# A two-layer diffusion trunk: token statistics of keys and queries apart, the scan's gate in its own pool, the attention's pools moved

## The chip, the cores and the metric

The kernel runs on one core of a Trainium2 chip. The metric is the device time of one execution in microseconds, as the median of the runs. A core has five engines that work through a queue of instructions each, in order: TensorE (PE: matmuls), VectorE (DVE), ScalarE (ACT), GpSimd (POOL) and SyncE (SP), which here only issues DMAs. They wait for one another by semaphores. GpSimd and ScalarE issue DMAs too.

## What is computed

Two layers of a trunk over 640 tokens: 512 latent tokens and 128 context tokens. Cut to the parts that the change touches:

```python
def trunk_layer(x, mod, p, ctx):
    h = modulate(x, shift1, scale1)            # RMS norm, scale, shift
    z = h @ p['w_in']                          # one projection, split by columns
    y_a = mixer_ssm(z[ssm])                    # A: state-space scan, both ways
    q = rmsnorm(rmsnorm(c_q) @ w_uq)           # B: low-rank queries, per-head norm, rotary
    k, v = rmsnorm([rmsnorm(ckv) @ w_uk, k_rope]), rmsnorm(ckv) @ w_uv
    y_b = softmax(q k^T) v
    y_c = mixer_gmlp(z[gmlp])                  # C: mixing within chunks of 128
    x = x + gate1 * (norm([y_a, y_b, y_c]) @ w_out)
    x = x + gate2 * conv_ffn(modulate(x, shift2, scale2))

def mixer_ssm(u):                              # ... scan -> y
    y = gelu(y + d * u)
    return y * sigmoid(y @ ssm_w_glu)
```

The two rmsnorms of `c_q` (256 wide) and `ckv` (128 wide) give one scale for each token. These are the "token statistics": a sum of squares over the width, and its inverse square root.

## The kernel before

The whole trunk is one program on one core. An activation is kept transposed, channels on the partitions and the 640 tokens (642 columns with two of padding) along the free dimension, and cut in two halves of 322 and 320 columns. Matmuls are made of three passes (`whi*hh`, `whi*hl`, `wlo*hh`): ScalarE casts a weight tile to its high part `whi` (L117), VectorE subtracts for the low part `wlo` (L118). Each layer has two stretches: the mixers (0 to 464 us and 1010 to 1340) and the FFN (464 to 1010 and 1340 to 1800).

No order is written out by hand. A scheduler of the framework takes the program, simulates it, and lays down one fixed instruction order for each engine. Tiles live in pools; a pool opened where another was closed reuses its memory, and its first writes wait until the last readers and writers of what lay there are done. Each layer has two sides of the memory, `sa` and `sb`, on which pools are stacked.

The end of the mixer stretch, in the order of the code:

- The scan, in four quarters (`ssm_quarter`, once for each quarter of the channel groups). For each, GpSimd's queue loads its tables (`T` L692, `we` L690, `tp` L696, `qt` L694), GpSimd copies the state into `E` (L724, L727), VectorE scans (`m`, `H`, `hq`, L744 to L763), TensorE forms `y` (L775 to L777), ScalarE copies it to `ys` (L779), and SP stores it with two DMAs to `Yd` in memory (L781).
- The gate (`ssm_output`), in the scan's pool: it loads `yT`, transposed, back from `Yd` with 16 DMAs, 8 on SP and 8 on GpSimd in turn (L800), and for both halves `t` of its 256 channels takes a square on ScalarE (`ga`, L811), two operations on VectorE (L812, L813), a tanh (L814), one more on VectorE (L815) and two copies to `gl` (L819). Then TensorE multiplies by `wg` (`glu`, L824), ScalarE takes a tanh (`th`, L828), and VectorE writes `yA` (L829, L830).
- The projection for the attention, in the pool `prj` on side `sa`: `put_c` evicts three blocks of the input projection (`win`): for the keys' block (m = 4) `ckh`, `ckl`, `sqk`, for the queries' two (m = 2, 3) `cqh` (L977), `cql` (L978), `sqq` and `sq` (L980). Ten one-column matmuls `tst` (L1008) give the token sums; VectorE makes `v` (L1011, L1012), one inverse square root of 10 columns (`rsqrt`, L102 to L111), and two copies into `sc` (L1014, L1016).
- Six key/value tiles: TensorE `kv` (L1036 to L1038), ScalarE copies `ks` (L1040), squares `hsq` (L1042) and writes `Vt` scaled by `sc` (L1044); VectorE reduces `ms` (L1043). Then the key norms (L1151 to L1166), five query tiles `q` (L1055 to L1062) and the query norms, whose last product is L1189.
- The attention, in pools `att` and `actx` on side `sb`: transposes `kt`, `qt`, the casts `kh` (L1236) and `kl` (L1237), maxima `mx`, scores and values. In between TensorE works off the matmuls of the modulation (`mod`, L261), whose weights SP loads (`raw<-w_mod`, L258).

## Time and profile before

| what | us |
|---|---|
| median of 3 runs (1825.23 to 1832.4) | 1825.25 |
| the profiled execution | 1826.58 |
| its span | 1824.8 |
| TensorE busy | 1694.3 (93%) |
| VectorE busy | 1156.8 (63%) |
| ScalarE busy | 679.8 (37%) |
| GpSimd busy | 312.8 (17%) |
| TensorE busy in 0 to 464 (mixers, layer 0) | 387.85 of 464 |
| in 464 to 1010 (FFN, layer 0) | 535.58 of 546 |
| in 1010 to 1340 (mixers, layer 1) | 293.93 of 330 |
| in 1340 to 1800 (FFN, layer 1) | 457.48 of 460 |

A busy share is an average over stages: in the FFNs TensorE is nearly never idle, in the mixers it is at times. A row of a timeline gives start, duration, and in brackets the idle time before it and what ended it. The span is what the profiler sees of one execution, and the execution's own time is 1.78 us longer.

### The profile page before, as it was taken

The numbers are of one execution on the slowest core, as the hardware profiler recorded it, in microseconds if no ns is written. First come the engines' busy times: TensorE is split into PE (matmuls) and PEld (weight loads), VectorE is DVE, ScalarE is ACT, GpSimd is POOL, SyncE is SP. The second block draws the span as 40 slices with busy tenths as digits, with TensorE's granted clock in tenths as the row PEclk, the third lists the DMA queues.
The fourth block names the chain that finished last, engine by engine and source line by source line (L and its number), as shares of the span: only waits on it lengthen the run. The fifth ranks groups of instructions, "written<-read, shape, count | busy, mean of one in ns | idle before, by whom it ended". The sixth has DMA issues, their size and how long they took to land.

```text
span 1824.8 us, 28970 instructions
## 1 busy us (share of the span) xinstructions
PE 1694.3 (93%) x11248; PEld 1512.6 (83%) x11248; DVE 1156.8 (63%) x2421; ACT 679.8 (37%) x1210; POOL 312.8 (17%) x738
## 2 busy tenths in 40 slices
PE   5878889999989999999999888999989999999998
PEld 3767755468889999999999876455989999999998
DVE  6887875667674646556477568566786464555564
ACT  4334454433452414224244346343344232332241
POOL 2886200000086060540000120000000000000000
PEclk7889789899899999999999978999989999999999
DMA  9265453301443523234132633540223131331221
GB/s 281 84 174 148 124 162 123 110 15 56 129 137 118 170 56 116 59 94 116 35 90 67 164 105 107 167 133 1 70 70 93 36 104 47 93 92 36 82 82 58
DMA packets 217577, 182.48 MB, mean 100 GB/s; under 512 B 33438, under 2 KB 202204, under 8 KB 217440
## 3 DMA queue, kind: packets, MB, share of 16 engines
q1 hardware_dynamic: 194736, 154.33, 28.2%
q0 software_dynamic: 8272, 23.87, 4.4%
q10 hardware_dynamic: 14432, 2.44, 0.7%
q8 instruction: 89, 1.46, 0.3%
q14 instruction: 48, 0.39, 0.1%
HBM read 161.94 MB, written 18.64 MB: 99 GB/s over the span
## 4 chain that ended last, share of the span: by engine, by line
PE 75%; DVE 10%; DMA 7%; ACT 4%; POOL 2%; issue 2%; ACTq 1%; SPq 0%; DVEq 0%; POOLq 0%
PE up L141 11%; PE up L143 11%; PE up L142 11%; PE dn L142 6%; PE dn L141 6%; PE dn L143 6%; PE o L1287 3%; PE mod L261 2%; DMA raw<-w_mod 2%; PE wo L141 1%; PE wo L143 1%; PE wo L142 1%; DMA raw<-ffn_w_up 1%; PE s L1267 1%; PE win L141 1%
## 5 line engine op out<-in xcount | busy, mean ns | idle before, releaser
L141 PE MATMUL up<-hh,whi 128*128 128x322 f32 x1408 | 435.6, 315 | 8.8 <-ACT hh L357 7.9
L143 PE MATMUL up<-hh,wlo 128*128 128x322 f32 x1408 | 440.9, 314 | 1.1 <-DVE wlo L118 1.0
L142 PE MATMUL up<-hl,whi 128*128 128x322 f32 x1408 | 439.7, 313 | 1.6 <-DVE hl L358 1.5
L141 PEld LDWEIGHTS up<-hh,whi 128*128 128x128 f32 x1408 | 266.1, 191 | 14.3 <-ACT hh L357 7.2
L142 PEld LDWEIGHTS up<-hl,whi 128*128 128x128 f32 x1408 | 268.8, 191 | 2.6 <-DVE hl L358 2.6
L143 PEld LDWEIGHTS up<-hh,wlo 128*128 128x128 f32 x1408 | 267.9, 190 | 2.9 <-DVE wlo L118 1.9
L118 DVE TENSOR_TENSOR wlo<-raw,whi 128x1024 fp32r<-128x1024 f32 (+1 forms) x116 | 146.7, 1266 | 142.2 <-ACT whi L117 141.0
L142 PE MATMUL dn<-glo,dh 128*128 128x322 f32 (+1 forms) x704 | 218.5, 312 | 0.2 <-DVE glo L118 0.2
L143 PE MATMUL dn<-gh,dl 128*128 128x322 f32 (+1 forms) x704 | 217.9, 311 | 0.0
L141 PE MATMUL dn<-gh,dh 128*128 128x322 f32 (+1 forms) x704 | 209.4, 312 | 4.5 <-DVE xT L1501 2.9
L1501 DVE SCALAR_TENSOR_TENSOR xT<-dn,mod,xT 128x320 f32<-128x320 f32 (+2 forms) x288 | 112.2, 435 | 129.5 <-PE dn L143 129.3
L117 ACT CAST whi<-raw 128x1024 fp32r<-128x1024 f32 (+1 forms) x116 | 120.5, 1040 | 151.1 <-PE up L142 56.8
L1532 ACT ACTIVATE cv<-up,prm,cw 128x321 f32<-128x321 f32 x88 | 54.3, 619 | 252.5 <-PE up L143 252.3
L141 PEld LDWEIGHTS dn<-gh,dh 128*128 128x128 f32 x704 | 131.0, 190 | 5.3 <-DVE xT L1501 3.1
L142 PEld LDWEIGHTS dn<-glo,dh 128*128 128x128 f32 x704 | 133.2, 189 | 0.5 <-DVE glo L118 0.5
L143 PEld LDWEIGHTS dn<-gh,dl 128*128 128x128 f32 x704 | 133.5, 190 | 0.0
L1533 DVE SCALAR_TENSOR_TENSOR cv<-up,cw,cv 128x320 f32<-128x320 f32 x88 | 48.3, 549 | 67.5 <-ACT cv L1532 67.5
L261 PE MATMUL mod<-raw,sT 128*32 128x256 f32 x768 | 64.5, 431 | 27.1 <-DMA raw<-w_mod 24.8
L118 DVE TENSOR_TENSOR dl<-raw,dh 128x1024 fp32r<-128x1024 f32 x44 | 54.0, 1227 | 45.8 <-ACT dh L117 45.6
L117 ACT CAST dh<-raw 128x1024 fp32r<-128x1024 f32 x44 | 46.1, 1047 | 56.8 <-DMA raw<-ffn_w_down 50.1
L261 PEld LDWEIGHTS mod<-raw,sT 128*32 128x32 f32 x768 | 19.5, 114 | 57.5 <-DMA raw<-w_mod 29.2
L1250 DVE TENSOR_REDUCE nml<-mx 128x1 f32<-128x640 f32 x64 | 50.9, 820 | 24.0 <-PE mx L1248 23.7
(472 smaller groups left out, 3422.5 us busy)
## 6 DMA issues: line engine op xcount, KB each, us to landing
raw<-w_mod SPq DMA_DIRECT2D x96, 512.0 KB, 4.6
raw<-ffn_w_up SPq DMA_DIRECT2D x88, 512.0 KB, 4.1
raw<-ffn_w_down SPq DMA_DIRECT2D x44, 512.0 KB, 3.5
raw<-w_in SPq DMA_DIRECT2D x10, 512.0 KB, 5.7
we<-WEd POOLq DMA_DIRECT2D x8, 512.0 KB, 4.1
qt<-Qd POOLq DMA_DIRECT2D x8, 512.0 KB, 5.1
raw<-w_out SPq DMA_DIRECT2D x16, 256.0 KB, 5.1
raw<-w_out SPq DMA_DIRECT2D x8, 512.0 KB, 3.4
```

What stands on the lines that cost most here:

```text
L117: self.nc.scalar.copy(hi, raw)
L118: self.nc.vector.tensor_tensor(lo, raw, hi.bitcast(F32), op=OP.subtract)
L141: mm(ps, wh, xh, start=start, stop=False)
L142: mm(ps, wh, xl, start=False, stop=False)
L143: mm(ps, wl, xh, start=False, stop=stop)
L261: nc.tensor.matmul(ps[j * 32:j * 32 + 32, c0:c0 + 256], self.sT[:, k0 + j, :], rv[:, j, :], start=k0 == 0, stop=k0 == 4)
L1250: V.tensor_reduce(nm[:, tt:tt + 1], pb[:, :, :320], axis=AX.XY, op=OP.max, negate=True)
L1267: mm(ps, kh[i][:, kc_], qh[i], start=True, stop=False)
L1287: mm(pb[i * 64:(i + 1) * 64, 0], Vt[:, kt, 2 * p + i], Ps[i][kt], start=kt == 0, stop=kt == 4)
L1501: self.nc.vector.scalar_tensor_tensor(self.xT[:, m, a:b], po[:, a - lo:b - lo], self.modcol(l, gi, m, c), self.xT[:, m, a:b], op0=OP.mult, ...
L1532: A.activation(z[:, 0:321], po[:, 0:321], AF.Identity, bias=b, scale=c1)
L1533: V.scalar_tensor_tensor(z[:, 1:321], po[:, 0:320], c0, z[:, 1:321], op0=OP.mult, op1=OP.add)
```

## The change

1. `rsqrt` makes its first guess with one operation, a multiplication of the bits by -0.5, in place of a shift and a multiplication. It takes an engine for its three Newton steps; GpSimd needs four operations for a step where VectorE needs three.
2. `token_scales` takes the place of the ten matmuls and the one call: keys and queries have five matmuls, a `v` and a first guess on VectorE each, and 12 Newton operations and one copy into `sc` on GpSimd each, right behind their blocks of the projection.
3. The gate gets a pool of its own, `so`, opened after the scan's pool is closed. Its code is called right after the scan in both layers; the tanh is written in place.
4. `att` and `actx` lie on the other side of the memory, `sa`, over `prj`.

```diff
@@ -95,20 +95,25 @@
         eng.tensor_tensor(o_re, o_re, t[0], op=OP.subtract)
         eng.tensor_tensor(o_im, o_im, t[1], op=OP.add)
 
-    def rsqrt(self, v, n):
-        nc = self.nc
-        sh = self.smt([128, n], f"rs_sh{n}", I32)
-        nc.vector.tensor_scalar(sh, v.bitcast(I32), 1, None, op0=OP.logical_shift_right)
-        y0 = self.smt([128, n], f"rs_y0{n}", I32)
-        nc.vector.tensor_scalar(y0, sh, -1.0, float(0x5F3759DF), op0=OP.mult, op1=OP.add)
+    def rsqrt(self, v, n, E=None):
+        E = E or self.nc.vector
+        n_ = f"{n}" if E is self.nc.vector else f"{n}p"
+        y0 = self.smt([128, n], f"rs_y0{n_}", I32)
+        self.nc.vector.tensor_scalar(y0, v.bitcast(I32), -0.5, float(0x5F3759DF), op0=OP.mult, op1=OP.add)
         cur = y0.bitcast(F32)
-        t = self.smt([128, n], f"rs_t{n}")
-        y = self.smt([128, n], f"rs_y{n}", bufs=3)
+        t = self.smt([128, n], f"rs_t{n_}")
+        y = self.smt([128, n], f"rs_y{n_}", bufs=3)
         for _ in range(3):
-            nc.vector.tensor_tensor(t, cur, cur, op=OP.mult)
-            nc.vector.scalar_tensor_tensor(t, t, -0.5, v, op0=OP.mult, op1=OP.mult)
-            nc.vector.scalar_tensor_tensor(y, t, 1.5, cur, op0=OP.add, op1=OP.mult)
+            E.tensor_tensor(t, cur, cur, op=OP.mult)
+            if E is self.nc.vector:
+                E.scalar_tensor_tensor(t, t, -0.5, v, op0=OP.mult, op1=OP.mult)
+                E.scalar_tensor_tensor(y, t, 1.5, cur, op0=OP.add, op1=OP.mult)
+            else:
+                E.tensor_tensor(t, t, v, op=OP.mult)
+                E.tensor_scalar(t, t, -0.5, 1.5, op0=OP.mult, op1=OP.add)
+                E.tensor_tensor(y, t, cur, op=OP.mult)
             cur = y
         return y
 
@@ -795,24 +800,23 @@
 
         nc, V, I = self.nc, self.nc.vector, self.I
         n = 8 * NC
-        y = pool.tile([128, 2, 8, NC], F32, name=self.uid("yT"), tag="uT", bufs=1)
+        y = pool.tile([128, 2, 8, NC], F32, name=self.uid("yT"), tag="yT", bufs=1)
         for g in range(16):
             (nc.gpsimd if g % 2 else nc.sync).dma_start(
                 out=y[(g % 8) * 16:(g % 8) * 16 + 16, g // 8],
                 in_=self.Yd[l][g].rearrange("(i c) k -> c i k", c=16))
-        wg = pool.tile([128, 2, 256], F32, name=self.uid("wg"), tag="tp", bufs=1)
+        wg = pool.tile([128, 2, 256], F32, name=self.uid("wg"), tag="wg", bufs=1)
         nc.sync.dma_start(out=wg, in_=I["ssm_w_glu"][l].rearrange("(t p) n -> p t n", t=2))
-        g = [pool.tile([128, NT], F32, name=self.uid("gl"), tag=tg, bufs=1) for tg in ("E", "R")]
+        g = [pool.tile([128, NT], F32, name=self.uid("gl"), tag=tg, bufs=1) for tg in ("g0", "g1")]
         for t in range(2):
             yv = y[:, t].rearrange("p i k -> p (i k)")
             nc.gpsimd.memset(g[t][:, 512:CX], 0.0)
-            a = pool.tile([128, n], F32, name=self.uid("ga"), tag="m1", bufs=1)
-            b = pool.tile([128, n], F32, name=self.uid("gb"), tag="m2", bufs=1)
+            a = pool.tile([128, n], F32, name=self.uid("ga"), tag="ga", bufs=1)
             nc.scalar.activation(a, yv, AF.Square)
             V.tensor_scalar(a, a, 0.044715, 1.0, op0=OP.mult, op1=OP.add)
             V.tensor_tensor(a, a, yv, op=OP.mult)
-            nc.scalar.activation(b, a, AF.Tanh, scale=math.sqrt(2.0 / math.pi))
-            V.scalar_tensor_tensor(a, b, 1.0, yv, op0=OP.add, op1=OP.mult)
+            nc.scalar.activation(a, a, AF.Tanh, scale=math.sqrt(2.0 / math.pi))
+            V.scalar_tensor_tensor(a, a, 1.0, yv, op0=OP.add, op1=OP.mult)
             av = a.rearrange("p (i k) -> p k i", i=8)
             for k0, k1, c in ((0, 64, 0), (65, 81, CX)):
                 o = g[t][:, c:c + 8 * (k1 - k0)].rearrange("p (k i) -> p k i", i=8)
@@ -824,7 +828,7 @@
                     nc.tensor.matmul(ps[s][:, :hi - lo], wg[:, t, m * 128:(m + 1) * 128],
                                      g[t][:, lo:hi], start=t == 0, stop=t == 1)
             for s, (lo, hi) in enumerate(((0, 320), (320, NT))):
-                th = pool.tile([128, 322], F32, name=self.uid("th"), tag="H", bufs=1)
+                th = pool.tile([128, 322], F32, name=self.uid("th"), tag="th", bufs=1)
                 nc.scalar.activation(th[:, :hi - lo], ps[s][:, :hi - lo], AF.Tanh, scale=0.5)
                 V.tensor_scalar(th[:, :hi - lo], th[:, :hi - lo], 1.0, 0.5, op0=OP.add, op1=OP.mult)
                 V.tensor_tensor(yA[:, m, lo:hi], th[:, :hi - lo], g[m][:, lo:hi], op=OP.mult)
@@ -931,7 +935,6 @@
                 self.ssm_quarter(l, q, ssm, tables or self.ssm_load(l, q, ssm), U, st, hq)
                 tables = None
             self.ssm_states(l, st)
-            self.ssm_output(l, ssm, yA)
 
         if l > 0:
             scans(tables)
@@ -954,6 +957,9 @@
             tb_ctx.close()
             self.params(1)
             scans(None)
+        ssm_ctx.close()
+        with tc.tile_pool(name=f"so{l}", bufs=1, side=sb) as so:
+            self.ssm_output(l, so, yA)
 
 
         vt = late.enter_context(tc.tile_pool(name=f"vt{l}", bufs=1, side=sa))
@@ -988,11 +994,26 @@
                 if s == 1:
                     A.activation(ckx, po[:, CX - lo:NT - lo], AF.Copy, scale=g)
 
+        def token_scales(sq, width, o, nm):
+            ps = self.pa("tst")
+            for i in range(5):
+                nc.tensor.matmul(ps[:, i:i + 1], sq[:, TOK[i]:TOK[i] + 128], self.ones[:, 0:1],
+                                 start=True, stop=True)
+            v = self.smt([128, 5], nm)
+            V.tensor_scalar(v, ps[:, 0:5], 1.0 / width, EPS, op0=OP.mult, op1=OP.add)
+            CH.tensor_copy(sc[:, o:o + 5], self.rsqrt(v, 5, CH))
+        CH = nc.gpsimd
+        CH.memset(sc[:, 5:6], 1.0)
         for m in (4, 2, 3):
             w = in_load(m)
             for s in range(2):
                 in_half(m, w, s, put_c)
+            if m == 4:
+                token_scales(sqk, 128, 6, "vk")
         V.tensor_tensor(sqq, sqq, sq2, op=OP.add)
+        token_scales(sqq, 256, 0, "vq")
 
         cc = pt("cc", [128, 128])
         nc.sync.dma_start(out=cc, in_=I["cache_ckv"][0, l])
@@ -1001,19 +1022,6 @@
         self.tr(ps[:, :128], cc)
         A.copy(ckh[:, :128], ps[:, :128])
         V.tensor_tensor(ckl[:, :128], ps[:, :128], ckh[:, :128].bitcast(F32), op=OP.subtract)
-        ps = self.pa("tst")
-        for i in range(5):
-            for j, s in enumerate((sqq, sqk)):
-                nc.tensor.matmul(ps[:, j * 5 + i:j * 5 + i + 1], s[:, TOK[i]:TOK[i] + 128],
-                                 self.ones[:, 0:1], start=True, stop=True)
-        v = self.smt([128, 10], "v10")
-        V.tensor_scalar(v[:, 0:5], ps[:, 0:5], 1.0 / 256, EPS, op0=OP.mult, op1=OP.add)
-        V.tensor_scalar(v[:, 5:10], ps[:, 5:10], 1.0 / 128, EPS, op0=OP.mult, op1=OP.add)
-        r10 = self.rsqrt(v, 10)
-        V.tensor_copy(sc[:, 0:5], r10[:, 0:5])
-        V.memset(sc[:, 5:6], 1.0)
-        V.tensor_copy(sc[:, 6:11], r10[:, 5:10])
 
         ps = self.pa("ckvo")
         self.tr(ps[:, :128], ckx)
@@ -1066,13 +1074,12 @@
         for _ in range(5):
             next(fill, None)
         prj.close()
-        ssm_ctx.close()
 
 
         yb = late.enter_context(tc.tile_pool(name=f"yb{l}", bufs=1, side=sa))
         yB = yb.tile([128, 4, NT], F32, name=self.uid("yB"), tag="yB")
         with ExitStack() as es:
-            at = es.enter_context(tc.tile_pool(name=f"att{l}", bufs=1, side=sb))
+            at = es.enter_context(tc.tile_pool(name=f"att{l}", bufs=1, side=sa))
             yh, yl = self.attention(l, M, yb, at, es, qs, ks, Vt, yB, yA, yc, ssc, fill)
         FH = self.later.enter_context(tc.tile_pool(name=f"fh{l}", bufs=1, side=sb))
         n2 = ExitStack()
@@ -1294,7 +1301,7 @@
             yield
 
 
-        with self.tc.tile_pool(name=f"actx{l}", bufs=1, side=self.sides[1]) as cx:
+        with self.tc.tile_pool(name=f"actx{l}", bufs=1, side=self.sides[0]) as cx:
             qc, kc = t("qc", [104, 8, 128], pool=cx), t("kc", [104, 8, 128], pool=cx)
             nc.sync.dma_start(out=kc[96:104].rearrange("p h c -> p (h c)"), in_=self.I["k_onehot"])
             for src, dst, g in ((qs[:, 4], qc, qg), (ks[:, 5], kc, kg)):
```

ScalarE in layer 1, where the third block's first half (320 columns) has been evicted; `cqh` and `sq` belong to the projection, `ga`, `gb` and `gl` to the gate, `ks` to the key/value tiles. Before:

```order
L977 ACTIVATE cqh_11114<-win_11251,prm_2004 128x320
L980 ACTIVATE sq_1657_11121<-win_11251 128x320
L811 ACTIVATE ga_10759<-yT_10737 128x648
L1040 COPY ks_11352<-kv_11382 128x8x64
L117 CAST whi_11484<-raw_11483 128x768
L977 ACTIVATE cqh_11114<-win_11251,prm_2004 128x322
```

and now:

```order
L983 ACTIVATE cqh_11112<-win_11275,prm_1998 128x320
L815 ACTIVATE ga_11059<-yT_11037 128x648
L986 ACTIVATE sq_1644_11119<-win_11275 128x320
L818 ACTIVATE ga_11059<-ga_11059 128x648
L823 ACTIVATE gl_11056<-ga_11059 128x512
L823 ACTIVATE gl_11056<-ga_11059 128x128
L122 CAST whi_11499<-raw_11498 128x768
L983 ACTIVATE cqh_11112<-win_11275,prm_1998 128x322
L815 ACTIVATE ga_11068<-yT_11037 128x648
```

The gate's square now stands ahead of `sq`, and the first key/value eviction has moved behind the whole gate.

SP in layer 1, around the last `Yd` stores (`x2`: two in a row). Before:

```order
L781 DMA Yd_306<-ys_10651 128x2x81 x2
L134 DMA raw_11489<-w_uq 128x768
L800 DMA yT_10737<-Yd_306 16x8x81 x2
L781 DMA Yd_306<-ys_10727 128x2x81 x2
L791 DMA out_new_ssm_re<-sto_10733 32x64
L791 DMA out_new_ssm_im<-sto_10733 32x64
L800 DMA yT_10737<-Yd_306 16x8x81 x6
```

and now:

```order
L786 DMA Yd_306<-ys_10648 128x2x81 x2
L139 DMA raw_11504<-w_uq 128x768
L786 DMA Yd_306<-ys_10724 128x2x81 x2
L796 DMA out_new_ssm_re<-sto_10730 32x64
L796 DMA out_new_ssm_im<-sto_10730 32x64
L805 DMA yT_11037<-Yd_306 16x8x81 x8
```

Two loads that stood ahead of the last stores stand behind them.

GpSimd in layer 0, between quarters 2 and 3 of the scan (`rs_t5p`, `rs_y5p`, `vq`: the queries' Newton steps). Before:

```order
L692 DMA T_2259<-Td_290 128x656
L767 COPY st_706<-hq_2028 128x2x2
L727 COPY E_2265<-h_117 128x4
L767 COPY st_706<-hq_2028 128x2x2
L696 DMA tp_2263<-Wd_298 128x512
L694 DMA qt_2261<-Qd_282 128x1024
```

and now, the last Newton step and what follows:

```order
L109 TENSOR_TENSOR rs_t5p_2641<-rs_y5p_2642 128x5
L114 TENSOR_TENSOR rs_t5p_2641<-rs_t5p_2641,vq_2637 128x5
L115 TENSOR_SCALAR rs_t5p_2641<-rs_t5p_2641 128x5
L116 TENSOR_TENSOR rs_y5p_2642<-rs_t5p_2641,rs_y5p_2642 128x5
L1005 COPY sc_703<-rs_y5p_2642 128x5
L701 DMA tp_2257<-Wd_298 128x512
L699 DMA qt_2255<-Qd_282 128x1024
L732 COPY E_2259<-h_117 128x4
```

The Newton chain has come ahead of the `tp` and `qt` loads of quarter 3, and the copy into `E` has moved behind them.

## Rows read from the trace of the kernel before

**Rows 1.** Windows: length, busy us of each engine, clock, DMA share, GB/s.
```profile
560.00:970.00 410.00, 409.20 (x2879) 403.23 (x2877) 232.37 (x403) 138.74 (x208) 100.70 (x180) 1.00 0.31 91
1080.00:1100.00 20.00, 16.55 (x54) 13.18 (x55) 11.42 (x35) 12.83 (x24) 0.00 (x0) 0.66 0.12 40
```

**Rows 2.** SP's timeline in layer 1: start, us, instruction, [idle before <-releaser].
```profile
1069.56 0.89 SPq L781 DMA_DIRECT2D Yd<-ys  x2
1071.50 5.34 SPq L800 DMA_DIRECT2D yT<-Yd  x6
```

**Rows 3.** GpSimd's timeline in layer 1.
```profile
1075.15 1.05 POOL L800 DMA_DIRECT2D yT<-Yd  x2 [3.11 <-DMA Yd<-ys]
1106.53 0.52 POOL L1214 MEMSET ql<- 1x512 f32 x1 [30.33 <-DVE ms L1153]
```

**Rows 4.** DMA issues, 1060 to 1080: count, KB each, median us to landing.
```profile
yT<-Yd POOLq DMA_DIRECT2D x8, 40.5 KB, 4.8
```

**Rows 5.** The tile yT in layer 1, its 16 loads.
```profile
DMA to landing us min/median/max: 1.9/4.5/5.5
```

**Rows 6.** ScalarE's timeline in layer 1.
```profile
1077.95 0.75 ACT L811 ACTIVATE ga<-yT 128x648 f32<-128x648 f32 x1 [2.02 <-DMA yT<-Yd]
...
1083.29 1.43 ACT L819 ACTIVATE gl<-ga 128x512 f32<-128x512 f32 x2 [0.36 <-DVE ga L815]
...
1095.02 0.58 ACT L1040 COPY ks<-kv 128x512 f32<-128x512 f32 x1 [5.08 <-PE kv L1038]
...
1103.80 0.60 ACT L1042 ACTIVATE hsq<-kv 128x512 f32<-128x512 f32 x1
1104.29 0.69 ACT L1044 ACTIVATE Vt<-kv,sc 128x512 f32<-128x512 f32 x1
```

**Rows 7.** TensorE's timeline in layer 1.
```profile
1075.97 0.41 PE L141 MATMUL win<-hh,whi 128*128 128x322 f32 x1 [0.27 <-ACT sq L980]
...
1082.98 0.80 PE L1036 MATMUL kv<-whi,ckh 128*128 128x512 f32 x1 [3.19 <-ACT sq L980]
```

**Rows 8.** VectorE's timeline in layer 1.
```profile
1107.12 0.58 DVE L102 TENSOR_SCALAR rs_sh<-ms 128x48 int32<-128x48 int32 x1
...
1121.25 0.75 DVE L1237 SCALAR_TENSOR_TENSOR kl<-kt,kg,kh 96x512 fp32r<-96x512 f32 x1
...
1135.96 0.68 DVE L1189 TENSOR_TENSOR qs<-qx,qx 128x512 f32<-128x512 f32 x1
1138.11 0.69 DVE L1358 TENSOR_TENSOR ac<-ac,msq 128x512 f32<-128x512 f32 x1 [1.46 <-ACT msq L1357]
```

**Rows 9.** GpSimd's timeline in layer 0.
```profile
200.31 0.19 POOL L727 COPY E<-h 128x4 f32<-128x4 f32 x1 [0.42 <-ACT E L720]
...
204.14 0.54 POOL L696 DMA_DIRECT2D tp<-Wd  x1 [3.52 <-PE y L775]
...
218.31 0.53 POOL L800 DMA_DIRECT2D yT<-Yd  x1 [1.21 <-DMA Yd<-ys]
```

**Rows 10.** VectorE's timeline in layer 0.
```profile
190.34 0.17 DVE L109 TENSOR_TENSOR rs_t<-rs_y 128x10 f32<-128x10 f32 x1
...
201.01 0.84 DVE L744 TENSOR_TENSOR m<-E,T 128x656 f32<-128x656 f32 x1 [0.63 <-DMA T<-Td]
...
215.62 0.69 DVE L1043 TENSOR_REDUCE ms<-hsq 128x8 f32<-128x512 f32 x1 [4.55 <-ACT hsq L1042]
...
229.14 0.49 DVE L812 TENSOR_SCALAR ga<-ga 128x648 f32<-128x648 f32 x1
...
229.66 0.83 DVE L813 TENSOR_TENSOR ga<-ga,yT 128x648 f32<-128x648 f32 x1
```

**Rows 11.** The chain that ended last, in layer 0: start, us, what.
```profile
204.99 5.16 DMA qt<-Qd
...
243.89 3.55 DMA raw<-w_mod
```

**Rows 12.** GpSimd's timeline in layer 1, the scan's last quarter.
```profile
1051.71 2.34 POOL L724 COPY E<-h 128x4 f32<-128x4 f32 x1 [3.29 <-DVE H L752]
```

## The prediction

> **What bounds the kernel now.** I read the windows by stage first. In the middle of layer 0's FFN, 560 to 970 us, TensorE is busy 409.20 of 410 us at full clock [rows 1]: the FFNs' code is unchanged, and nothing here can shorten that. What can move are the two mixer stretches, and in them the end, where scan, gate, key/value projection and query projection meet: about 196 to 270 us in layer 0 and 1068 to 1146 us in layer 1. There TensorE has gaps: 16.55 us busy of 20 in 1080 to 1100, at a granted clock of 0.66 [rows 1].
>
> In layer 1 I follow TensorE's waits backwards. It stops once for 3.19 us, on ScalarE's square of the third block's second half [rows 7]; ScalarE had been held up by the gate's first square, which waited 2.02 us for yT [rows 6]. From 1095.02 to 1104.98 ScalarE sets the pace: it evicts key/value and glu tiles [rows 6]. Then VectorE has hardly a gap until the last query product ends at 1135.96 + 0.68 = 1136.64 [rows 8]. In layer 0 the chain that ended last goes through a qt load of 5.16 us, then VectorE, and from 243.89 us through w_mod loads [rows 11].
>
> **The change, part by part.**
>
> *Shift dropped from rsqrt.* One VectorE operation less per call. In layer 1's VectorE-bound stretch that is the 48-wide one, 0.58 us [rows 8], and one of each small query call, which I estimate at 0.18 from the small operations of rows 10: 0.94 us saved. Elsewhere VectorE waits, and it is worth nothing.
>
> *Newton steps on GpSimd.* One 10-wide call (11 operations of 0.17 us [rows 10], 0.2 with the gaps, and two copies) leaves VectorE; two 5-wide chains of 12 + 1 come to GpSimd. In layer 1 they cost nothing: GpSimd does nothing between its last yT load at 1075.15 and a memset 30.33 us later [rows 3], so two chains of 13 x 0.2 = 2.6 us lie in that idle time, and the first V eviction that needs the scales comes later than they do. In layer 0 the queries' chain stands on GpSimd ahead of the tp and qt loads of quarter 3. Before, GpSimd sat idle 3.52 us ahead of that tp load, until TensorE's y of quarter 2 [rows 9]; 2.6 us fit in. If that cover is gone, they fall on the qt load of the chain. On VectorE the scan of quarter 2 loses some ten interleaved Newton operations, 10 x 0.2 = 2 us, and y of quarter 2 waited for that scan.
>
> *E copy behind two loads.* GpSimd's second copy of the state into E for quarter 3, at 200.31 us before, stands behind the tp and qt loads now [rows 9], which wait for y of quarter 2. So the scan of quarter 3, which began at 201.01 us [rows 10], begins at about 204 + 0.5 + 0.5 (two issues) - 2 (the earlier scan of quarter 2) = 203: y of quarter 3 comes up to 2 us later. Key/value and query matmuls now stand ahead of it on TensorE, so only the gate waits for it.
>
> *Gate in its own pool.* Its memory is free when the whole scan pool is closed, and that pool holds ys, which the last Yd store reads. So all 16 yT loads wait for that store; before, most went ahead of it, and only SP's and GpSimd's last two waited. In layer 1 SP issues the last stores from 1069.56 [rows 2], and they have landed at 1075.1, where GpSimd's last two loads were released [rows 3]. GpSimd needs 0.53 us a load (1.05 for two), so its fourth, the last of the gate's first half, starts at 1075.15 + 3 x 0.53 = 1076.7. Loads on its queue landed 4.8 us after the issue [rows 4], the quickest of all after 1.9 and the slowest after 5.5 [rows 5]. So y is there at 1078.6 to 1082.2; I take 1081.5, by 4.8, since eight loads of the same size are again queued there: +3.5 us on the 1077.95 of rows 6.
>
> What stands behind it is the worse part. On ScalarE the gate's square `ga` stands ahead of the square `sq` of the third block's first half; before, behind it. TensorE's next 24 win matmuls wait for `sq`. They started at 1075.97 [rows 7]; now at 1081.5 + 0.75 + 0.45 = 1082.7, and the first key/value matmuls have moved behind the gate's second half. ScalarE's queue then reads: tanh, gl pair, cast, cqh, second ga, sq, tanh, gl pair, and only then evictions. With 0.75 for ga and for the tanh over the same columns, 1.43 for a gl pair [rows 6], estimates of 0.8 for the cast, 0.5 each for cqh and sq, and about 2.1 on VectorE for each half (three passes over 648 columns at the 0.49 to 0.83 of such passes, [rows 10]), the second half's gl are done 11.4 to 13 us after y, and the first key/value tile 2.5 to 3.5 after that. Six tiles of 0.58 + 0.60 + 0.69 = 1.87 us are 11.2; glu tanh and ckt add some 2.3: last V eviction at 1081.5 + 27.4 to 30 = 1108.9 to 1111.5, instead of 1104.98 [rows 6]. I take the middle, 1110.2, **+5.2**; with the ends of y's landing it is +1 to +7.2.
>
> *Attention's pools over the projection's memory.* kh, kl, ql and the memsets wait no longer for the gate but for the last readers of the projection's tiles, the product at L1189 the last of them. VectorE's four kl operations (0.75 the first, 2.2 in all) leave the stretch ahead of it [rows 8]: VectorE's end moves by +5.2 - 0.94 - 2.2 = +2.1. Behind it kl, four kh evictions and six memsets (0.52 the first [rows 3], 3.6 in all) are new ahead of the max matmuls. VectorE had 1.46 us idle there [rows 8], and TensorE other work; I charge +1, between nothing and 2.2 (kl whole). Layer 1: **+3.1 us**, from +1 - 3.1 = -2.1 to +7.2 - 0.94 + 2.2 = +8.5.
>
> In layer 0 the pieces weigh otherwise. Key/value evictions no longer straddle y of quarter 3: VectorE waited 4.55 us for the last key tile, until 215.62 [rows 10]. If key norms start up to that much earlier, the VectorE work behind them shifts too. Against it the gate: Yd of quarter 3 had landed at 218.31 [rows 9], now up to 2 us later; with 1.6 us for the loads ahead and 4.8 to land, y is there near 226. VectorE took up the gate at 229.14, busy with keys until then [rows 10]: the gate is hidden unless key norms gain over 3 us, and then it holds the queries' evictions behind it on ScalarE. I take **-1 us**, from -5.5 (4.55 and 0.94, all kept) to +4 (2.6 for GpSimd's chain and 1.4 of the gate).
>
> **A rule against it.** GpSimd's copy of four columns into E took 2.34 us while VectorE was at its scan [rows 12], and 0.19 in another place [rows 9]. So a tiny GpSimd operation can be held up. The Trainium skill, "SBUF — State Buffer", section "Who interferes with whom", says that a VectorE instruction with two SBUF inputs and a GpSimd instruction that reads SBUF exclude each other for a whole instruction. The long row agrees with that, the short one shows that it need not happen. What it would do here: if each of the 13 operations of layer 0's chain waited for a scan operation of 0.84 us [rows 10], the chain would take 11 us in place of 2.6, and tp, qt and the gate of that layer would come 11 - 3.5 - 1.5 (GpSimd's gaps there) = 6 us late.
>
> **Rivals.** *A, the freed VectorE wins (faster).* The loads land quickly, ScalarE's new order costs nothing, and both layers keep their savings: layer 1 -0.94 - 2.2 - 1 (the V eviction that waited for the scales' 10-wide call), layer 0 -5.5: -9.6, and 1815.6. For it speaks that ScalarE idled 2.02 us ahead of `ga` anyway; against it that ScalarE's order is fixed and no yT load can start before 1075.1. *B, the gate's square blocks ScalarE (slower).* Both layers at their worst, +8.5 + 4 = +12.5: 1837.8. It decides from where y lands over 4 us after ScalarE has reached the square; the 4.8 of rows 4 is near that. *C, GpSimd's chain is held up by the scan.* +6 in layer 0 in place of -1: 1834.4. *D, it does nothing:* layer 0 goes on through w_mod loads (3.55 us the first of four waits, [rows 11]) and swallows its gain, layer 1's terms cancel: 1825.2.
>
> **How the numbers follow.** The profiled execution took 1826.58 (span 1824.8 and 1.78 around it), 1.33 over the median of 1825.25. 1826.58 + 3.1 - 1 = 1828.7; as a median, less 1.33, **1827.4**. The forecast's own bounds: 1825.25 - 7.6 and + 12.5, 1817.6 to 1837.8. Chances: forecast 0.37, D 0.12, A 0.24, B 0.19, C 0.08. Eight in ten: 1812 to 1838 (A with some 3 us beyond its price, B to its price). A measurement of this kernel tells about 0.5%, 9.1 us, from no change. Faster by more: nearly all of A, 0.22; slower by more: most of B and half of C, 0.21; within: 0.57.
>
> **What would show it.** In layer 1 ScalarE's first `ga` at 1079 to 1082.2, TensorE stopped for some 5 us ahead of the win matmuls behind it, the last V eviction 4 to 6.5 us later than before, the product at L1189 some 2 us later. In layer 0 tp of quarter 3 not later than 204.1, key norms ahead of 216, GpSimd's Newton operations near 0.2 us each. It is wrong if that chain takes over 5 us, if the gate's square in layer 0 begins after 228, if `ga` of layer 1 begins ahead of 1078.6, or if the query products end earlier than before in both layers.

## The result, and the profile after

The changed kernel takes 1846.29 us (median of 6 runs, 1838.47 to 1850.28), the kernel before beside it 1828.11: ratio 1.0099, 95% interval 1.0081 to 1.0117. The forecast of 1827.4 failed, and the time lies outside its range of 1812 to 1838. The profiled execution, the fastest of the six, took 1838.47 us (span 1836.7); before's took 1826.58 (span 1824.8). So the trace explains 11.9 us, and the medians differ by 18.2. A second profile of the same kernel (experiment e8) has a span of 1841.3; its runs give 1.0071 (1.0045 to 1.0098).

The loss splits at the first `win` matmul of layer 1: it comes 2.5 us later than before (7.2 in e8), and from there the first matmul of layer 1's FFN is 8.7 us later (8.8 in e8). Layer 1's loss is thus the same in both profiles; layer 0's isn't.

Layer 1 first. The two windows of [rows 1], and three windows of the stretch in question (length, busy us of PE, PEld, DVE, ACT, POOL, clock, DMA share, GB/s):

```profile
560.00:970.00 410.00, 410.00 (x2884) 404.20 (x2883) 229.88 (x399) 136.63 (x204) 102.64 (x183) 1.00 0.31 92
1080.00:1100.00 20.00, 12.22 (x49) 9.98 (x50) 9.65 (x20) 9.44 (x17) 9.00 (x32) 0.78 0.38 92
...
1084.00:1088.00 4.00, 4.00 (x17) 4.00 (x18) 1.67 (x3) 2.17 (x3) 2.54 (x8) 0.57 0.49 123
1088.00:1092.00 4.00, 2.28 (x13) 1.61 (x11) 2.01 (x5) 2.33 (x4) 0.00 (x0) 1.00 0.02 1
...
1097.00:1102.00 5.00, 5.00 (x14) 3.73 (x13) 1.78 (x6) 1.31 (x4) 1.65 (x7) 0.54 0.04 13
```

In the same 20 us TensorE now works 12.22 instead of 16.55 us. The loads come as forecast. SP's timeline in layer 1 (start, us, instruction), answering [rows 2]:

```profile
1072.88 0.87 SPq L786 DMA_DIRECT2D Yd<-ys  x2
...
1077.30 3.64 SPq L805 DMA_DIRECT2D yT<-Yd  x8
```

All eight loads wait for the last Yd store. GpSimd's timeline in layer 1, answering [rows 3]; the short rows are of the two Newton chains:

```profile
1077.83 4.21 POOL L805 DMA_DIRECT2D yT<-Yd  x8 [9.34 <-ACT cqh L983]
...
1082.71 0.19 POOL L115 TENSOR_SCALAR rs_t5p<-rs_t5p 128x5 f32<-128x5 f32 x1
...
1084.15 0.78 POOL L115 TENSOR_SCALAR rs_t5p<-rs_t5p 128x5 f32<-128x5 f32 x1
...
1098.93 0.19 POOL L1005 COPY sc<-rs_y5p 128x5 f32<-128x5 f32 x1
1145.07 0.52 POOL L1221 MEMSET ql<- 1x512 f32 x1 [45.95 <-DVE qs L1196]
```

ScalarE's timeline, answering [rows 6]:

```profile
1082.73 0.74 ACT L815 ACTIVATE ga<-yT 128x648 f32<-128x648 f32 x1 [2.25 <-POOL rs_t5p L114]
1083.38 0.42 ACT L986 ACTIVATE sq<-win 128x320 f32<-128x320 f32 x1
...
1094.63 1.37 ACT L823 ACTIVATE gl<-ga 128x512 f32<-128x512 f32 x2 [1.13 <-DVE ga L819]
...
1101.83 0.59 ACT L1048 COPY ks<-kv 128x512 f32<-128x512 f32 x1 [2.57 <-PE kv L1046]
...
1114.56 0.69 ACT L1052 ACTIVATE Vt<-kv,sc 128x512 f32<-128x512 f32 x1
```

The releaser in the first row is doubtful (the chain of waits has a yT load there, 1079.42 + 2.93). `sq` stands behind `ga`, and no key/value eviction comes before 1101.83. TensorE's timeline, answering [rows 7]:

```profile
1083.85 0.41 PE L146 MATMUL win<-hh,whi 128*128 128x322 f32 x1 [3.94 <-ACT sq L986]
...
1093.51 1.28 PE L1001 MATMUL tst<-ones,sqq 128*128 128x1 f32 x10 [3.23 <-DVE sqq L1015]
...
1098.11 0.78 PE L1044 MATMUL kv<-whi,ckh 128*128 128x512 f32 x1
```

It stops for 3.94 us ahead of `win`, comes back at a granted clock of 0.57 (near the lower of its two levels, 1.2 GHz), stops again for 3.23 us, and begins the key/value matmuls at 1098.11, at a clock of 0.54. VectorE's timeline, answering [rows 8]:

```profile
1129.84 0.95 DVE L1070 TENSOR_REDUCE ms<-hsq 128x8 f32<-128x768 f32 x1 [0.93 <-ACT hsq L1069]
...
1144.09 0.68 DVE L1196 TENSOR_TENSOR qs<-qx,qx 128x512 f32<-128x512 f32 x1
1145.74 1.40 DVE L1244 SCALAR_TENSOR_TENSOR kl<-kt,kg,kh 96x512 fp32r<-96x512 f32 x2 [0.97 <-ACT kh L1243]
```

Layer 0. GpSimd's timeline there, answering [rows 9]:

```profile
198.28 0.33 POOL L109 TENSOR_TENSOR rs_t5p<-rs_y05p 128x5 f32<-128x5 f32 x1
...
202.25 0.19 POOL L1005 COPY sc<-rs_y5p 128x5 f32<-128x5 f32 x1
205.27 0.59 POOL L701 DMA_DIRECT2D tp<-Wd  x1 [2.82 <-PE y L781]
205.86 0.54 POOL L699 DMA_DIRECT2D qt<-Qd  x1
206.39 0.20 POOL L732 COPY E<-h 128x4 f32<-128x4 f32 x1
...
225.13 4.22 POOL L805 DMA_DIRECT2D yT<-Yd  x8 [7.50 <-ACT hsq L1069]
```

VectorE's timeline in layer 0, answering [rows 10]:

```profile
203.25 0.69 DVE L1051 TENSOR_REDUCE ms<-hsq 128x8 f32<-128x512 f32 x1 [3.50 <-ACT hsq L1050]
...
206.63 0.84 DVE L749 TENSOR_TENSOR m<-E,T 128x656 f32<-128x656 f32 x1 [1.34 <-POOL E L732]
...
231.15 0.50 DVE L816 TENSOR_SCALAR ga<-ga 128x648 f32<-128x648 f32 x1 [3.47 <-ACT ga L815]
```

ScalarE's timeline in layer 0:

```profile
230.38 0.74 ACT L815 ACTIVATE ga<-yT 128x648 f32<-128x648 f32 x1 [2.16 <-DMA yT<-Yd]
231.03 0.79 ACT L1069 ACTIVATE hsq<-q 128x768 f32<-128x768 f32 x1
```

The chain that ended last, in layer 0 (start, us, what), answering [rows 11]:

```profile
227.78 2.58 DMA yT<-Yd
...
248.30 4.78 DMA raw<-w_mod
```

The E copy of quarter 3 moved from 200.31 to 206.39, its scan from 201.01 to 206.63. The gate's square waits 2.16 us for yT, and a square of the queries stands right behind it; VectorE waits 3.47 us for that first square.

### The profile page after: what moved, and what is told of

Read it like the earlier page. It is cut to its first block, busy times and chain, and to the rows that moved or that the text cites. A ratio compares the mean times of both kernels' runs of the same rounds, so it can differ in the third digit from the quotient of the medians.

```text
span 1836.7 us, 28995 instructions
## 1 busy us (share of the span) xinstructions
PE 1692.4 (92%) x11248; PEld 1509.0 (82%) x11248; DVE 1150.8 (63%) x2377; ACT 678.8 (37%) x1210; POOL 323.8 (18%) x792
## 4 chain that ended last, share of the span: by engine, by line
PE 73%; DMA 9%; DVE 8%; ACT 5%; POOL 2%; issue 1%; ACTq 1%; SPq 0%; DVEq 0%; POOLq 0%
PE up L146 11%; PE up L148 10%; PE up L147 10%; PE dn L147 5%; PE dn L148 5%; PE dn L146 5%; DMA raw<-w_mod 2%; PE o L1294 2%; PE mod L266 2%; DMA raw<-ffn_w_up 1%; PE wo L146 1%; PE wo L148 1%; PE wo L147 1%; PE s L1274 1%; PE win L146 1%
```

## Experiments

The questions were which of the three parts costs, whether late loads or the order on ScalarE and TensorE is the mechanism in layer 1, and whether the move of the Newton steps is worth anything. The lines under each kernel are its edit, cut to what matters (e5 and e6 are the kernel before with part 3 or part 4 of the change). Last come two tables of profiles.

**One part left out, or alone.** e1: the changed kernel with the gate back in the scan's pool. e2: with the attention's pools back. e3, e5 and e6: the kernel before with the token part, the gate's pool or the attention's pools alone.

```diff
e1, e3   -        with tc.tile_pool(name=f"so{l}", bufs=1, side=sb) as so:
         +            self.ssm_output(l, ssm, yA)      # tags uT, tp, E, R, m1, m2, H as before
e2, e3   -  at = es.enter_context(tc.tile_pool(name=f"att{l}", bufs=1, side=sa))
         +  at = es.enter_context(tc.tile_pool(name=f"att{l}", bufs=1, side=sb))    # actx likewise
```

> The changed kernel with the gate back in the scan's pool (that pool closed after the projection again); token statistics and the attention's pools stay changed. The changed kernel's profiled execution was 11.9 us longer than that of before, and its median 18 us. Theory G (the gate's own pool makes all 16 yT loads wait for the last Yd store, the gate's square blocks ScalarE, key/value evictions end late): it gets back the 5 to 8 us by which the last V eviction of layer 1 came late, so about 1829 to 1833, with ScalarE's first ga of layer 1 ahead of or close behind 1078 and the last V eviction near 1105. Theory A (the attention's pools over the projection's memory cost most): it stays within 3 us of the changed kernel, 1838 or more.

Measured: 1833.22 us, 1.0014 (0.9989 to 1.0039). Without the gate's pool most of the loss is gone. But it is not gone in the way that theory G wants: the last V eviction is still 4.3 us late against the layer's start, and the key/value evictions stand behind both halves of the gate here too (the second half's `gl` end at 1096.6, the first key eviction begins at 1099.3).

> The changed kernel with the attention's two pools back on the side where they were; gate pool and token statistics stay changed. Theory A: kh, kl and their memsets no longer wait for the last query product, and the 4.3 us by which the first max of layer 1 was later than the query products explain, with 2 to 3 us of layer 0, come back: 1831 to 1834. Theory G: the last V eviction stays at about 1115 and no more than 4 us come back: 1834 to 1840.

Measured: 1840.78 us, 1.0072 (1.0053 to 1.0090). It stays slower, just above the range of both theories.

> The kernel before with the token statistics apart, their Newton steps on GpSimd, and the shift dropped; gate and attention pools as before. Both theories hold this part for harmless: within 4 us of before, 1822 to 1829. Rival C (GpSimd's chain is held up by VectorE and delays tp and qt of layer 0's last quarter): 5 us or more slower than before, with operations of 0.5 us or more in that chain.

Measured: 1821.88 us, 0.9977 (0.9955 to 0.9998): the only kernel of this study whose interval lies below 1, and it ends just there; of thirteen versions one may do that by chance.

> The kernel before with only the gate's own pool (opened after the scan's pool is closed, the tanh in place). From the runs so far: token statistics alone 0.9977 of before, token and gate 1.0072, so theory G wants the gate alone at about 1.0095, 1840 to 1848. If the gate's pool hurts only together with the reordered token statistics, it lies within 6 us of before.

Measured: 1833.52 us, 1.0035 (1.0014 to 1.0057). That is under the 1840 of theory G, and within the 6 us that stood for the gate hurting only together with the token part; the profiled execution, 6 us above the median, is one of the longer ones. In it the first gate square of layer 1 is 1.7 us later than before, counted from the layer's start, the last query product 9.0. So the gate's pool costs there without the rest, and in a way of its own: the key products on VectorE stand behind the first reduction of the queries, which comes late (before, it had come at 1109.22, between the keys' small operations). VectorE's timeline in layer 1 of e5:

```profile
1122.09 0.95 DVE L1063 TENSOR_REDUCE ms<-hsq 128x8 f32<-128x768 f32 x1 [4.77 <-ACT hsq L1062]
1122.96 0.20 DVE L1157 TENSOR_TENSOR Rs<-rs_y,sc 128x48 f32<-128x48 f32 x1
1123.08 1.75 DVE L1163 TENSOR_TENSOR ks<-krg,rs_y 128x1536 f32<-128x1536 f32 x1
```

> The kernel before with only the attention's two pools on the other side. Token and attention pools together were 1.0014, token alone 0.9977: if the parts add, 1.0037, 1832 to 1836. The changed kernel's layer 1 shows 4 us between the last query product and the max; theory A wants that gap here too. If the move only costs together with the gate's pool, it is within 3 us of before.

Measured: 1832.31 us, 1.0022 (1.0001 to 1.0043). VectorE's timeline in layer 1 of e6:

```profile
1139.40 0.68 DVE L1189 TENSOR_TENSOR qs<-qx,qx 128x512 f32<-128x512 f32 x1
1140.88 1.41 DVE L1237 SCALAR_TENSOR_TENSOR kl<-kt,kg,kh 96x512 fp32r<-96x512 f32 x2 [0.80 <-ACT kh L1236]
```

The `kl` operations have left the query stretch, which ends 1.9 us earlier, near the 2.2 that the prediction took. But from the last query product to the first max matmul it takes 6.4 us instead of 3.1, and at the first FFN matmul the kernel is 3.7 us behind. Not all parts add up: token -0.23% and gate +0.35 sum to +0.12, and measured together +0.72, clear of the intervals; token and attention sum to -0.01, and measured together +0.14, which is the same. All three sum to +0.34; together they cost 0.7 to 1.0.

**e4: the gate's pool opened while the scan's pool is still open**, so that its memory is free earlier.

```diff
-        ssm_ctx.close()
         with tc.tile_pool(name=f"so{l}", bufs=1, side=sb) as so:
             self.ssm_output(l, so, yA)
+        ssm_ctx.close()
```

> The changed kernel with one thing else: the gate's pool is opened while the scan's pool is still open, so it lies over other memory and its yT loads need no closed scan pool; the scan's pool is closed right behind the gate. Theory G: yT loads go out quarter by quarter again, the square of the gate waits less, and 5 us or more of the 12 come back (1833 or less). If the loss comes from the order that the scheduler lays down and not from the wait for the memory, it stays at 1838 or above.

Measured: 1922.57 us, 1.0527 (1.0506 to 1.0548). It doesn't answer the question. ScalarE's timeline in layer 0 of e4:

```profile
237.19 0.44 ACT L832 ACTIVATE th<-glu 128x322 f32<-128x322 f32 x1 [1.27 <-PE glu L828]
238.62 0.53 ACT L989 ACTIVATE ckh<-win,prm 128x320 fp32r<-128x320 f32 x1 [0.99 <-DVE yA L834]
```

The projection's first eviction waited for the gate's last product, so the gate's pool must now lie where the projection's tiles stand afterwards; the last `win` matmul of layer 0 came 85 us late. It shows what such an overlap costs.

**e7: e3, with the Newton steps left on VectorE. e10: the kernel before with the one 10-wide call, its Newton steps and copies on GpSimd and the shift dropped. e11: the kernel before with the shift dropped and nothing else.**

```diff
e7    -        CH = nc.gpsimd
      +        CH = nc.vector
e10   -        r10 = self.rsqrt(v, 10)
      +        r10 = self.rsqrt(v, 10, nc.gpsimd)
e11   -        nc.vector.tensor_scalar(sh, v.bitcast(I32), 1, None, op0=OP.logical_shift_right)
      -        nc.vector.tensor_scalar(y0, sh, -1.0, float(0x5F3759DF), op0=OP.mult, op1=OP.add)
      +        nc.vector.tensor_scalar(y0, v.bitcast(I32), -0.5, float(0x5F3759DF), op0=OP.mult, op1=OP.add)
```

> Token statistics apart and the shift dropped, gate and attention pools as before, but the Newton steps on VectorE. With them on GpSimd it was 0.9977. If the gain comes from GpSimd taking 24 operations a layer from VectorE, it is lost here: 1.000 or more, 1826 to 1832. If it comes from the earlier key statistics and the shorter call, it stays: 0.996 to 0.999.

Measured: 1839.58 us, 1.0063 (1.0039 to 1.0087), 0.86% above e3. At the last query product of layer 0 e7 is 2.3 us behind e3, at the end of that layer's attention 12.7, where no operation of the two chains stands. So most of the difference lies outside the stretch that the Newton steps relieve, and the run doesn't price that relief; between 255 and 290 us TensorE's granted clock is 0.86 in e7's profile, 0.98 in before's and 1.00 in e3's, which goes with it but wasn't tested.

> The ten token sums and the one 10-wide call as before, but its Newton steps and copies on GpSimd, and the shift dropped; gate and attention pools as before. Split and on GpSimd it was 0.9977, split and on VectorE 1.0063. If GpSimd's relief of VectorE is the gain, this is 0.996 to 0.999. If the gain needs the earlier key statistics, it is 1.000 or more.

Measured: 1826.64 us, 0.9992 (0.9973 to 1.0011): no difference, and between the two branches of the expectation, so it decides neither.

> The kernel before with the shift dropped from rsqrt, nothing else: VectorE has 22 operations less in each layer's calls. By the rows 0.94 us in layer 1 and less in layer 0: 1823 to 1827, the same as before within what can be measured. A time off by over 5 us either way would show that the order that the scheduler lays down, and not the operations, makes such differences.

Measured: 1843.66 us, 1.0090 (1.0068 to 1.0111). One operation less in each call (the trace of before has 22 of them in all, 11 a layer, and not 22 a layer) makes the kernel slower. The operation itself can't do that; the instructions are ordered anew. In layer 0 the last `win` matmul comes 10.3 us late and the first FFN matmul 10.0. In layer 1, TensorE's longest wait between 1000 and 1130 us in e11 (for what; us in total, times, longest) is one that before didn't have there:

```profile
PE cct L145 <- DMA cc<-cache_ckv: 6.1, 1, 6.1
```

**e9: late loads alone.** In the kernel before, yT takes the place of `ys`, so that all 16 loads wait for the last Yd store, as in the changed kernel; on ScalarE the order in layer 1 stays.

```diff
-        ys = t("ys", [128, 2, 2, NC])
+        ys = t("ys", [128, 4, 2, 2, NC])[:, 0]
-        y = pool.tile([128, 2, 8, NC], F32, name=self.uid("yT"), tag="uT", bufs=1)
+        y = pool.tile([128, 2, 8, NC], F32, name=self.uid("yT"), tag="ys", bufs=1)
```

> The kernel before with one thing else: yT lies in the place of ys, so all 16 loads of yT wait for the last Yd stores as they do with the gate's own pool; the pools and the token statistics are those of before, and on ScalarE the square sq still stands ahead of the gate's square, the first key/value eviction right behind it. The gate's pool alone gave 1.0035 (8.5 us in layer 1 of the profiled execution). If the late loads are what costs, this gives 1.003 to 1.006 with 5 us or more in layer 1. If it is the order on ScalarE and TensorE that the pool brings (gate ahead of sq, key/value tiles behind the gate), this stays within 3 us of before.

Measured: 1830.81 us, 1.0022 (0.9999 to 1.0046), and 0.4 us at layer 1's first FFN matmul. In layer 0 the order didn't stay (its last `win` matmul comes 20.7 us later). SP's eight loads begin together, as after:

```profile
1076.16 3.66 SPq L800 DMA_DIRECT2D yT<-Yd  x8
```

ScalarE's timeline in layer 1 of e9 shows `sq` ahead of `ga`, and a key eviction right behind it. But `ga` itself comes no later than before (-0.1 against the layer's start), so this run prices late loads, not a late square.

```profile
1078.00 0.44 ACT L980 ACTIVATE sq<-win 128x320 f32<-128x320 f32 x1 [0.62 <-DVE cql L978]
1081.13 0.74 ACT L811 ACTIVATE ga<-yT 128x648 f32<-128x648 f32 x1 [2.70 <-DMA yT<-Yd]
1082.19 0.59 ACT L1040 COPY ks<-kv 128x512 f32<-128x512 f32 x1 [0.31 <-PE win L142]
```

**e8: the changed kernel once more**, with no edit.

> The changed kernel once more, as it is. Its six executions ran from 1838.5 to 1850.3, and the one that was profiled was the quickest. If the rest of the time sits in a stretch that the profiled execution had at full clock, a second profile near 1846 shows a lower granted clock there; else the two profiles agree in every stage within 2 us.

Measured: 1842.41 us, 1.0071 (1.0045 to 1.0098). Its profile loses 7.2 us up to layer 1's start and 8.8 behind it, as told above.

**The order alone.** e12: the changed kernel, in layer 1 with a bias of zero, made from `sq`'s first half, on the gate's square, so that the square stands behind `sq`; in the code the gate's call moves behind the projection. e13: the same with `sq`'s second half; the first key/value evictions then come ahead of the gate's second `gl`. e14: e13 with the attention's pools back.

```diff
+            zero = pool.tile([128, 1], F32, name=self.uid("gz"), tag="gz", bufs=1)
+            nc.scalar.activation(zero, after, AF.Copy, scale=0.0)
-            nc.scalar.activation(a, yv, AF.Square)
+            nc.scalar.activation(a, yv, AF.Square, bias=zero)
```

> The changed kernel with one dependency more, in layer 1 only: the gate's square takes a zero bias that is made from sq of the third block's first half, so the scheduler lays sq ahead of the gate's square on ScalarE. Memory, loads and layer 0 stay those of the changed kernel; the key/value evictions stay behind the whole gate. The late loads alone cost nothing in layer 1, the gate's pool 8.5 us. If it is the sq behind the square that stops TensorE (3.9 us, and half clock after it), 3 to 6 us of the changed kernel's 8.7 in layer 1 come back: 1834 to 1842. If the evictions behind the gate are the cause, less than 2 us come back.

Measured: 1838.02 us, 1.0042 (1.0020 to 1.0063). The last V eviction is 2.3 us earlier than in the changed kernel, and the first max matmul 5.4 us earlier, but the attention gives it back, and the FFN starts 8.9 us late. By the median the expectation's first branch holds, by layer 1's FFN the second. From the first max to the first FFN matmul TensorE has the same 1081 matmuls as in before and in e1; they take 195.5 us at a granted clock of 0.97 in before, 200.0 at 0.94 in e12 and 191.0 at 0.99 in e1. What sets that clock wasn't tested.

> The same with the zero made from sq of the second half: the whole projection is ahead of the gate on ScalarE, and the first key/value evictions stand between the gate's two halves. If the order on ScalarE is the whole cause of layer 1's loss ahead of the query products (the last V eviction 7.9 us late against the layer's start), that eviction comes 5 to 8 us earlier than in the changed kernel; the 4 us behind the query products (attention's pools) stay. 1832 to 1840. If it makes no difference, layer 1's loss lies elsewhere (the w_mod loads between the key/value matmuls).

Measured: 1836.62 us, 1.0047 (1.0022 to 1.0073). ScalarE's timeline in layer 1 of e13, from the second half's square on:

```profile
1097.92 0.83 ACT L820 ACTIVATE ga<-yT,gz 128x648 f32<-128x648 f32 x1
1099.60 0.59 ACT L1057 COPY ks<-kv 128x512 f32<-128x512 f32 x1 [0.85 <-PE kv L1055]
...
1102.15 0.69 ACT L1061 ACTIVATE Vt<-kv,sc 128x512 f32<-128x512 f32 x1
1102.72 1.44 ACT L828 ACTIVATE gl<-ga 128x512 f32<-128x512 f32 x2
```

The gate's first square is 7.2 us later than before, more than in the changed kernel (2.3), and still 7.3 of the 8.7 us are back, also the 4 us behind the query products that were expected to stay. The medians alone don't tell e13 from e8 (1.0071); the reading rests on layer 1 in one profile of each.

> The kernel of e13 with the attention's pools back on their old side as well. If the order on ScalarE and the kh/kl casts behind the query products are the two causes in layer 1, this loses no more than 2 us there against before: 1824 to 1833. If a third cause is left, 1836 or more.

Measured: 1833.92 us, 1.0028 (1.0004 to 1.0052). Layer 1 now reaches its FFN 0.7 us earlier than in the kernel before. The whole kernel is still slower, by layer 0 (+7.0).

Profiles against the one of before, us. The first row is the first `win` matmul of layer 1; the others count from it, so they hold layer 1 alone.

```
                       after   e8    e2    e1    e3    e5    e6    e9   e12   e13   e14
layer 1 begins         +2.5  +7.2  +7.5  +4.0  -6.0  +4.0  +5.3  +3.3  +2.3  +7.0  +7.0
first gate square      +2.3  +2.6  +3.6  +1.0  +7.8  +1.7  -0.1  -0.1  +2.9  +7.2  +7.5
last win matmul        +7.0  +7.3  +8.1  +3.1  +1.6  +0.8  -0.0  -0.8  +3.4  +2.2  +2.5
last V eviction        +7.8  +7.9  +8.7  +4.3  +0.8  +3.9  -0.1  -1.5  +5.6  +1.4  +1.5
last query product     +5.7  +5.6  +8.1  +4.6  +0.5  +9.0  -1.9  -0.6  +3.5  -0.6  +1.2
first max matmul       +9.9  +9.9  +8.3  +5.7  +0.6  +9.0  +1.4  -0.6  +4.5  +0.2  +1.2
first FFN matmul       +8.7  +8.8  +5.7  +1.2  -0.0  +8.6  +3.7  +0.4  +8.9  +1.4  -0.7
```

And layer 0, against before: what the token part, the gate's pool and the attention's pools do alone and together.

```
                         e3 (token)  e5 (gate)  e2 (token, gate)  e1 (token, att)  after   e8
last y matmul              +6.5        +0.4         +6.5              +10.8         +7.7  +9.4
first yT load on GpSimd    +6.1        +5.5        +11.4              +10.4        +12.3 +14.3
last query matmul          +0.1        -1.0         +4.0               +4.3         +4.8  +6.8
first FFN matmul           -2.6        -1.2         +4.1               -0.3         +2.7  +6.4
```

## Why the prediction was wrong

The sum of +3.1 in layer 1 and -1 in layer 0 came out as +8.7 and +2.5, with +0.7 behind layer 1's first FFN matmul. Three steps failed: the way from the gate to the first key eviction in layer 1, TensorE's "other work" behind the query products, and the whole of layer 0, where y came much later than forecast and the gate wasn't hidden.

*Shift dropped (-0.94).* The operation is gone, but 0.58 was not its own price. The 48-wide shift ran beside GpSimd's memsets [rows 3, rows 8]; in the changed kernel these stand behind the query products (1145.07), and the 48-wide operation that is left takes 0.19 us, not 0.58. e11 shows besides that a term taken operation by operation has no standing of its own here: the new order is worth +0.9%. The saving can't be read apart.

*Newton steps on GpSimd (nothing).* Right. The chain of layer 0 takes 4.2 us (198.28 to 202.44), not 2.6, with two state copies in it, but tp still waits 2.82 us for TensorE behind it. In layer 1 the chains end at 1087.1 and 1099.1, ahead of the first V eviction at 1103.71.

*The rule against it.* Each of the four chains of the two layers has 12 operations and a copy. Of these 52, 46 take 0.19 to 0.33 us, and six take 0.44 to 1.09. But 27 of the short ones ran while VectorE did nothing, ten of the 13 of layer 0's queries among them: VectorE had ended its scan and stood idle for 3.50 us until 203.25. Each of the six long ones lay under a VectorE instruction and ended some 0.05 us behind its end. For the one of 0.78 us at 1084.15, the row of VectorE's timeline is:

```profile
1084.04 0.83 DVE L817 TENSOR_TENSOR ga<-ga,yT 128x648 f32<-128x648 f32 x1
```

So a tiny GpSimd operation does wait for the rest of such an instruction here. The Trainium skill, "SBUF — State Buffer", "Who interferes with whom", would let them wait for a whole VectorE instruction; the long rows agree with that. Rival C failed because its condition did not come: the chain met VectorE's idle time, and not the scan.

*E copy behind two loads (scan at 203, y up to 2 later).* Wrong in size: scan at 206.63, y 7.7 later. I had credited 2 us for an earlier scan of quarter 2; instead tp left 1.1 us later than before, and E stood behind its two issues. From that scan to the end of y another 2.1 us went, with three key reductions of some 0.69 us between its operations. That only the gate waits for y held in e3, where it cost nothing. The gain that stood against it, key norms up to 4.55 us earlier, didn't come: the last key reduction is at 217.50, where it had been at 215.62.

*The gate in layer 0 (hidden).* This step failed. The token part makes y late, the gate's pool makes every load wait for y's last store, and the two add up on yT (+12.3). The gate's square then starts at 230.38, the prediction's own sign for being wrong (after 228), with a square of the queries behind it; the last query matmul is 4.8 us late. That the two parts together cause this is not shown: e1 has the gate's pool as before, and there y comes 10.8 us late, the gate's square starts at 231.06 and the last query matmul is 4.3 late; in e11, with the shift dropped alone, it is 5.9 late. Nor does it settle the layer, since e1 reaches its FFN 0.3 us early all the same. Of layer 0's forecast -1 (up to +4) came +2.5 and, in e8, +7.2; the cause of that stays open.

*The gate in layer 1 (last V eviction +5.2, at most +7.2).* Mechanism right, size short: +7.8. Counted without the 2.46 us by which the layer starts late, SP's loads begin at 1077.30 - 2.46 = 1074.8 (forecast 1075.1), `ga` at 1080.3 (1081.5; the load that it waited for landed after 2.93 us, not 4.8). From `ga` to the end of the second half's `gl` it takes 13.3 us (forecast 11.4 to 13), from the first key eviction to the last V eviction 13.4 (13.5). The missed term lies between: 5.8 us instead of 2.5 to 3.5, since glu and key/value matmuls ran near half clock with TensorE busy throughout. TensorE had just stood still twice; I had counted the stops as waits only, and not the clock behind them. The window from the second half's `gl` to the first key eviction, in the changed kernel and then in e12:

```profile
1096.00:1101.83 5.83, 5.83 (x14) 4.19 (x15) 2.08 (x7) 1.28 (x5) 2.32 (x11) 0.52 0.04 11
1094.51:1099.48 4.97, 4.97 (x13) 3.61 (x14) 2.16 (x7) 1.30 (x5) 2.13 (x10) 0.60 0.04 13
```

Length times clock is 3.0 in both, and 3.0 to 3.1 in e8 (5.7 at 0.54), e2 (5.5 at 0.56) and e7 (5.1 at 0.59), which have the same glu and key/value matmuls there. At full clock that makes some 3.0 us, an estimate from these windows, and within the forecast.

*What holds TensorE.* The prediction had two reasons, a late y and the order on ScalarE behind it, which it called the worse part; rival B let it hang on y. The order is the cause: the key/value evictions stand behind both halves of the gate. e13 has the gate's square later still and gets 7.3 of 8.7 us back, and in e3 the square is 7.8 us late, the first evictions stand ahead of the gate's second half, and layer 1 loses nothing. e1 shows the other side: the gate's pool is as before, the evictions stand behind the gate, and the last V eviction is 4.3 us late. e12 shows that `sq` ahead of `ga` isn't enough. This is shown up to the max matmuls; how much of a delay there reaches the FFN differs with the clock of the attention (4.5 us less in e1, 4.5 more in e12 than in before). B's point of decision (y over 4 us after ScalarE is ready) was wrong: ScalarE waited 2.25 us.

*VectorE's end (-3.1 against the V eviction).* -2.1: VectorE waited 0.93 us for a square that it did not wait for before.

*Attention's pools (+1 ahead of the max matmuls, at most 2.2).* Mis-sized in the changed kernel: +4.2 from the last query product to the first max matmul, and 3.3 in e6. I had priced VectorE's `kl` alone, while `kh` on ScalarE, `kl`, `qh` and `ql` all wait for the same last product, and follow one another. But e1, e12 and e13 have the same pools, and there it is +1.1, +1.0 and +0.8, near the forecast. What the changed kernel, e8 and e6 have besides is an order on TensorE, here in the changed kernel:

```profile
1149.41 2.79 PE L266 MATMUL mod<-raw,sT 128*32 128x256 f32 x24 [2.40 <-DVE ql L1237]
```

24 `mod` matmuls wait for `ql`, and the first max matmul stands behind them, at 1152.13. In e13 these 24 stand behind it, and it waits for `qh` alone:

```profile
1146.98 0.56 PE L1264 MATMUL mx<-kh,qh 96*128 96x320 f32 x2 [1.74 <-ACT qh L1245]
```

TensorE's other work, which I had counted as cover for the wait, came to stand between the wait and the max matmuls. No run moves these matmuls alone.

*The FFNs ("nothing here can shorten that").* Right for the middle of them and for the changed kernel, too strong as a rule: from the first FFN matmul of layer 0 to layer 1's start it takes 515.9 us before, 515.7 after, but 512.5 in e3 and 521.0 in e5. e3's gain of 6.0 is for 3.4 us of that kind.

*The rivals.* Rival B is nearest in price: +12.5, where the profiled execution came out at +11.9; it had 0.19. That is luck in part: its price was the sum of all upper ends, its account of y was wrong, and the median, 1846.29, lies 8.5 us above it. A and D needed layer 1's terms to cancel.

*Left open.* Why the median is another 8 us above the first profile. The two profiles of the changed kernel differ by 4.6 us, all of it before layer 1: 1.6 at layer 0's last `win` matmul, 3.7 at its first FFN matmul. TensorE's granted clock differs there; the window from 255 to 272 us in the changed kernel:

```profile
255.00:272.00 17.00, 11.15 (x111) 6.26 (x107) 9.44 (x20) 8.37 (x16) 3.27 (x6) 1.00 0.84 270
```

The same window in e8:

```profile
255.00:272.00 17.00, 13.39 (x105) 8.01 (x106) 10.23 (x22) 8.99 (x17) 3.27 (x6) 0.80 0.79 249
```

Over the whole span the six runs go from 1838.47 at a clock of 0.950 to 1850.28 at 0.943. That fits, but e8 runs some 2 us behind there, so that the two windows don't hold quite the same work, and what sets the clock in layer 0 wasn't tested. e12 and e13, whose layer 0 is written as in the changed kernel, begin layer 1 at +2.3 and +7.0. Layer 0's loss is known to some 5 us only.

## What to carry to other kernels

When a tile's memory moves, ask first what the move does to the order of a shared engine's queue: a gate's square 7 to 8 us late cost 0.8 to 1.4 us at the last V eviction where independent evictions stood ahead of the gate's end (e3, e13), and one 2.3 us late cost 7.8 us where they stood behind it. Price a wait of TensorE with the slower matmuls that follow it (here 5.8 us in place of some 3.0), and look at what stands behind a new common wait in each engine's queue, TensorE's too. Parts of a change under a scheduler need not add up, so run each alone: here the token part alone was the only version clear below the kernel before, if by 0.23% only. And when an operation is short, look at what the other engine did meanwhile before calling it free.
